# Making the head projections' weight sums on GpSimd from loaded blocks, and starting the MLP's sums and the second block's token loads later

## The chip, the cores and the metric

The kernel runs on one core of one Trainium2 chip. The metric is device time in microseconds of one execution; the median of three executions is 2469.45 us.

## The reference

One decoder layer on x of 2048 tokens by 1024 features in float32, then a final RMSNorm:

```python
h = rmsnorm(x, mix_norm_g[l])
proj = h @ w_in[l]
q, k, v, g, u = jnp.split(proj, [R, 2 * R, 3 * R, 4 * R], axis=-1)
y_ret = jax.nn.silu(g) * head_rmsnorm(retention(q, k, v, positions), ret_gn_g[l])
y_pool = pool_mixer(u, pool_w[l], pool_scale[l])
x = x + jnp.concatenate([y_ret, y_pool], axis=-1) @ w_out[l]
x = x + cross_attn(rmsnorm(x, xa_norm_g[l]), mem_n, xa_wq[l], xa_wkv[l], xa_wo[l])
x = x + conv_glu_ffn(rmsnorm(x, ffn_norm_g[l]), ffn_w_up[l], ffn_conv_w[l],
                     ffn_conv_b[l], ffn_w_down[l])
```

Retention has 4 heads of 128 (rotary q and k, decay, chunks of 128 tokens, a norm by head, a SiLU gate). The pooling mixer takes trailing means over 2, 4, 8 and 16 tokens in 4 groups. The cross-attention reads 256 memory tokens; the MLP has 2 x 2816 columns and a causal convolution of width 3 ahead of the gate.

## The kernel before

The sequence is worked through in two blocks of 1024 tokens (b = 0 and 1), features on the 128 partitions. A float32 matmul is made as three passes (`passes`, lines 271 to 273): each operand is split into a high part, which ScalarE writes (`act.activation` to the type fp32r), and a low part, which VectorE writes (the difference), and the passes are high by high, high by low and low by high. So every weight tile that TensorE reads is first loaded, then split by ScalarE and VectorE.

Projections with square blocks of weights use a scheme of seven products in place of eight. Three of the seven left operands are blocks of the weights, the other four are sums of blocks. For the head projections these are the arrays `Ad` (one entry for each of the 8 pairs of column groups in `PAIRS`), for the MLP `Ud` and `Dd`. `weight_sums` makes all of them in device memory, without any engine's arithmetic: GpSimd issues for each job four DMAs that copy and four that add while they write (lines 925 and 922). It is a generator; its jobs are advanced by turns, each with a small ScalarE copy (line 940) and a GpSimd copy (line 941) that tie the turn to a place in the order. `spacing` says how many calls make one turn. Turns are taken in the last steps of the prologue, between the value projections of block 0, in the head projections and in the later stages.

Block 0 then goes as follows. `folded_weights` (a generator, `todo` in the outer function, advanced by `folded(n)`) multiplies the attention's weights into the memory: first wkv and wqT (stores of `Md`, line 501), later pool weights and wo (stores of `WPd`, line 571, and `VWd`, line 591). `values` projects v. Beside it `rope_steps` makes the rotary tables on VectorE and ScalarE, and SP stores them (`rope0`, line 1903), and `quarter_sums` makes the sums of x for the seven products. `head_projections` makes q, k, the gates and the pool inputs: a `Heads` member for each pair fetches seven tiles of 128x512 (line 1020), into places of `raws` (seven places of 512 columns in R and S3), splits each (line 1636) into a place of `prs` (Q and S45) and multiplies it with a sum of x. It runs `retention` for the head before in between (`behind`), and `pool_steps` (`todo` inside it) for the pooled groups. What is left of both is done behind the last product (`finish()` and a loop), after which the outer function runs the rest of `folded`, four times with two `token_squares` of block 1 between (the second copy of x, `xR`, tokens on partitions; loaded by `load_tokens` at line 626, squared by ScalarE with a row sum at line 622). The output projection (`unit`, weights from `wout_r` and `WPd`) and the cross-attention follow.

Each engine runs its instructions in order. The written order is not that order: a scheduler with a model of time places each instruction on its engine, so that a change in one place can move rows elsewhere. SP issues most loads, in order, and a load waits in SP's queue until its place is free.

The head projections' fetch, and the rest behind block 0's heads:

```python
own = [sums[i][:, : halves * P] for i in range(4)]
self.loads = [part(0, 0), own[2], own[1], part(0, 1), own[0], own[3], part(1, 1)]
...
load_tokens(1, k, room)
folded(1)
for h in range(HEADS):
    for k in (2 * h, 2 * h + 1):
        token_squares(1, k, room, token_sums[:, KT:])
    folded(1)
```

Of the kernel before, what the change touches and what calls it, by code (L numbers as in the profile page):

```python
# [8 lines left out]
F32 = mybir.dt.float32  # L9
# [3 lines left out]
ALU = mybir.AluOpType  # L13
# [123 lines left out]
def trunk(ctx, tc, xT, xR, memT, pos, w_qkgu, w_v, wkv, wqT, wo, wout_r, wout_p, poolT, w_up, w_dn, vecs, consts, outT):  # L137
# [576 lines left out]
    def retention(b, h, qkg, v):  # L714
# [89 lines left out]
        yield  # L804
        a.mixed()
# [731 lines left out]
    def head_projections(b, v, rb, t1, t2, z, got):  # L1537
# [76 lines left out]
        class Heads(Member):  # L1614

            def __init__(self, p):
                super().__init__([w_qkgu[n] for n in PAIRS[p]], Ad[p], 0, 4)
                self.groups, self.how, self.seen, self.acc = PAIRS[p], [""] * 7, set(), None
                self.ended = []
# [68 lines left out]
        class Late:  # L1688
# [6 lines left out]

            def fetch(self, i):
# [49 lines left out]
        fetches, made, highs = list(items), [], []  # L1746
# [5 lines left out]
        def fill():  # L1752
# [3 lines left out]
            if len(made) < len(items) and prs.room():  # L1756
                m, i = items[len(made)]
                while i not in m.raw:
                    fetch()
# [5 lines left out]
        def step():  # L1765
            if todo and next(todo[0], True) is not None:
                todo.pop(0)

# [8 lines left out]
        for at, (m, i) in enumerate(items[:own]):  # L1777
# [18 lines left out]
            next(under[0], None)  # L1796
# [24 lines left out]
        S[0] = new_s(F32, 0)  # L1821
        raws = Places([(R, j * T) for j in range(3)] + [(r, 0) for r in S], T)
        prs = Places([(Q, j * T) for j in range(3)], T)
# [95 lines left out]
    for n in range(1, 2 * KT + HEADS):  # L1919
# [17 lines left out]
        if n > 2 * KT:  # L1937
            next(under[0])
        folded(1)
    reclaim(spare)  # L1940
    for b in range(NB):
# [9 lines left out]
        def between():  # L1951
            next(behind[0], None)
            place[0] += 1
            if b == 0 and place[0] % 2:
                next(under[0])
# [20 lines left out]
        else:  # L1976
# [28 lines left out]
        first = 0  # L2005
# [9 lines left out]
        for n in range(first, KT):  # L2015
# [4 lines left out]
            unit(raw, mixed, add_residual(b, n, xs, got=got), (0, 2, 3, 1, 4, 6, 7, 5) if b == 0 else range(KT))  # L2020
# [201 lines left out]
```

## Time and profile before

| what | us |
|---|---|
| median of three executions | 2469.45 (2468.44 to 2470.31) |
| the profiled execution's own time | 2470.04 |
| its span, first to last instruction | 2468.2 |
| TensorE busy in the span | 2403.8 (97%) |
| VectorE busy | 1717.3 (70%) |
| ScalarE busy | 1355.2 (55%) |
| GpSimd busy | 308.2 (12%) |
| bytes moved by DMA | 526.23 MB |

The span is what the trace holds; the execution's own time has 1.8 us more around it. PE is TensorE's matmuls, PEld its weight loads, DVE VectorE, ACT ScalarE, POOL GpSimd, SP the engine that issues most DMAs. A name with a q behind it is the engine's queue, which issues and waits. In a row of instructions, out<-in are tiles by name, and the bracket at the end holds the engine's idle time before it and what ended that.

### The profile page before, as it was taken

To read this page: it belongs to the slowest core of one execution; us is meant where nothing else is said; L and a number is where in the kernel's file an instruction comes from. 1 tells how busy PE (TensorE), PEld (TensorE's weight loads), DVE (VectorE), ACT (ScalarE), POOL (GpSimd) and SP (SyncE) were. 2 spreads that over 40 slices of the span, in tenths; PEclk is the share of its full clock that TensorE was granted. 3 is DMA by queue.
4 is the path that set the end of the run, shared out by engine and by line. 5 is a ranking of instruction groups with operands and counts; after the bars stand their busy time and mean duration, and the time that the engine had idled before them with its cause. 6 is when DMAs were issued, how large, how long until landed. Compare 5 with 4: busy or idle time off the path is not lost.

```text
span 2468.2 us, 33388 instructions
## 1 busy us (share of the span) xinstructions
PE 2403.8 (97%) x11186; PEld 2002.1 (81%) x11186; DVE 1717.3 (70%) x2872; ACT 1355.2 (55%) x2498; POOL 308.2 (12%) x477
## 2 busy tenths in 40 slices
PE   9779999999999999999999999999999999999998
PEld 8658877888888888888888888888888888888887
DVE  7366874564566775574678776897667688867876
ACT  7434565443345553434655555675555577666664
POOL 0245120315113300000000010020000000000000
PEclk9889998999999999999999999999999999999999
DMA  9999589949868744356568655665446468757952
GB/s 355 300 256 283 144 230 308 286 121 291 252 190 220 182 110 154 111 203 209 177 198 283 205 187 164 213 222 171 162 158 214 136 224 294 258 181 261 356 187 73
DMA packets 275581, 526.23 MB, mean 213 GB/s; under 512 B 30144, under 2 KB 59344, under 8 KB 275408
## 3 DMA queue, kind: packets, MB, share of 16 engines
q1 hardware_dynamic: 212768, 408.59, 49.7%
q0 software_dynamic: 37376, 86.00, 14.9%
q10 hardware_dynamic: 25264, 29.49, 3.4%
q8 instruction: 88, 1.44, 0.2%
q14 instruction: 85, 0.70, 0.1%
HBM read 420.68 MB, written 189.28 MB: 247 GB/s over the span
## 4 chain that ended last, share of the span: by engine, by line
PE 83%; DVE 1%; ACT 0%; issue 0%; DVEq 0%; ACTq 0%
PE mm L271 26%; PE mm L272 26%; PE mm L273 26%; PE aux L271 1%; PE aux L273 1%; PE aux L272 1%; PE aux L855 1%; DVE Z L243 0%; PE aux L363 0%; PE aux L765 0%; PE aux L763 0%; PE aux L735 0%; PE aux L747 0%; PE aux L778 0%; PE aux L737 0%; DVE T L243 0%
## 5 line engine op out<-in xcount | busy, mean ns | idle before, releaser
L271 PE MATMUL mm<-G,Q 128*128 128x512 f32 (+1 forms) x1665 | 642.1, 386 | 19.1 <-ACT Q L1636 10.4
L273 PE MATMUL mm<-G,Q 128*128 128x512 f32 (+1 forms) x1665 | 637.7, 385 | 2.3 <-DVE Q L243 2.3
L272 PE MATMUL mm<-G,Q 128*128 128x512 f32 (+1 forms) x1537 | 590.4, 384 | 0.4 <-DVE G L251 0.2
L272 PE MATMUL mm<-G,E 128*128 128x512 f32 (+1 forms) x1092 | 420.4, 385 | 0.0
L271 PE MATMUL mm<-G,E 128*128 128x512 f32 (+1 forms) x1092 | 418.8, 385 | 0.7 <-ACT E L259 0.7
L273 PE MATMUL mm<-G,E 128*128 128x512 f32 (+1 forms) x1092 | 418.3, 385 | 0.2 <-DVE E L243 0.2
L271 PEld LDWEIGHTS mm<-G,Q 128*128 128x128 f32 x1665 | 315.2, 189 | 84.0 <-ACT Q L1636 11.6
L273 PEld LDWEIGHTS mm<-G,Q 128*128 128x128 f32 x1665 | 314.8, 189 | 64.5 <-DVE Q L243 3.8
L272 PEld LDWEIGHTS mm<-G,Q 128*128 128x128 f32 x1537 | 291.1, 189 | 56.3 <-DVE G L243 1.2
L243 DVE TENSOR_TENSOR Z<-Z,mm 128x512 f32<-128x512 f32 (+1 forms) x322 | 215.0, 671 | 124.2 <-PE mm L273 122.7
L251 DVE SCALAR_TENSOR_TENSOR Z<-Z,vecs 128x1024 f32<-128x1024 f32 x176 | 224.4, 1279 | 50.2 <-ACT Z L1089 46.8
L271 PEld LDWEIGHTS mm<-G,E 128*128 128x128 f32 x1092 | 205.1, 188 | 41.9 <-ACT E L259 0.9
L273 PEld LDWEIGHTS mm<-G,E 128*128 128x128 f32 x1092 | 205.1, 188 | 41.5 <-DVE E L243 0.4
L272 PEld LDWEIGHTS mm<-G,E 128*128 128x128 f32 x1092 | 205.1, 188 | 41.1
L243 DVE TENSOR_TENSOR Q<-R,Q 128x512 fp32r<-128x512 f32 x180 | 122.5, 686 | 83.3 <-ACT Q L259 53.7
L1026 ACT ACTIVATE E<-R 128x512 fp32r<-128x512 f32 (+1 forms) x165 | 101.4, 615 | 141.1 <-PE mm L272 135.2
L243 DVE TENSOR_TENSOR T<-T 128x512 f32<-128x512 f32 (+4 forms) x196 | 134.1, 688 | 24.8 <-ACT T L432 12.4
L243 DVE TENSOR_TENSOR G<-T,G 128x512 fp32r<-128x512 f32 (+1 forms) x169 | 110.3, 672 | 38.4 <-ACT G L259 18.7
L973 ACT ACTIVATE G<-T 128x512 fp32r<-128x512 f32 x180 | 108.6, 623 | 40.5 <-DMA T<-Gd 30.4
L243 DVE TENSOR_TENSOR E<-R,E 128x512 fp32r<-128x512 f32 (+1 forms) x137 | 91.3, 671 | 54.9 <-ACT E L1026 39.3
L1089 ACT ACTIVATE Z<-Z,vecs 128x1024 f32<-128x1024 f32 x88 | 109.1, 1241 | 31.8 <-DVE Z L243 30.9
L1026 ACT ACTIVATE E<-S 128x512 fp32r<-128x512 f32 (+1 forms) x107 | 65.9, 616 | 106.7 <-PE mm L272 104.1
(348 smaller groups left out, 3917.8 us busy)
## 6 DMA issues: line engine op xcount, KB each, us to landing
T<-Gd SPq DMA_DIRECT2D x168, 256.0 KB, 4.7
Ud<-w_up POOLq DMA_DIRECT2D x132, 256.0 KB, 9.5
Gd<-Z SPq DMA_DIRECT2D x110, 256.0 KB, 2.8
R<-Ud SPq DMA_DIRECT2D x106, 256.0 KB, 2.7
R<-w_up SPq DMA_DIRECT2D x80, 256.0 KB, 3.1
S<-Ud SPq DMA_DIRECT2D x70, 256.0 KB, 2.9
Gd<-T SPq DMA_DIRECT2D x56, 256.0 KB, 3.3
T<-Xd SPq DMA_DIRECT2D x53, 256.0 KB, 4.1
```

Of the source, the lines that this page charges most:

```text
L243: return eng.tensor_tensor(out=out, in0=a, in1=b, op=op)
L251: return dve.scalar_tensor_tensor(out=out, in0=a, scalar=s, in1=b, op0=op0, op1=op1)
L271: pe.matmul(ps, lh, rh, start=start, stop=False, skip_group_check=more)
L272: pe.matmul(ps, lh, rl, start=False, stop=False, skip_group_check=more)
L273: latest[0] = pe.matmul(ps, ll, rh, start=False, stop=stop, skip_group_check=more)
L855: pe.transpose(tp[:, j * P : (j + 1) * P], e.f[:, j * P : (j + 1) * P], ident)
L973: one = act.activation(hi, x, AF.Copy, scale=-1.0 if i == 2 else 1.0)
L1026: act.activation(p2[:, 0, :w], self.raw[i].f[:, :w], AF.Copy)
L1089: act.activation(self.c[g].f, a[:, 2:], AF.Identity, bias=cb[:, f : f + 1], scale=cw[2][:, f : f + 1])
```

## The change

In block 0 the sums for the head projections are no longer taken from `Ad`. `Heads` loads the four raw blocks of a pair, and `summed` lets GpSimd add two places of `raws` into a third (for one sum in place), and store the sum to `Ad`, from where block 1 reads it as it did. `weight_sums` loses the eight jobs of `Ad`; the MLP's jobs, which stay, are not advanced in the prologue, in block 0's values or in its head projections any more. What is left of retention and of the pooled groups behind block 0's last product is interleaved with steps of `folded`; the places are set back to whole tiles ahead of that (`back`). The loads and squares of `xR` go into the loop of block 0's output projection, one for each unit. `retention` has one more `yield` ahead of the scores of heads 0 to 2, and one ahead of the last head's `mixed`. Block 0's output units take k = 3 last.

```diff
@@ retention
         both_ss, rr = small(8), small(8)
+        if h < HEADS - 1:
+            yield
...
         c.scaled(rr)
         yield
+        if h == HEADS - 1:
+            yield
         a.mixed()
@@ weight_sums
-        jobs = [((w_qkgu[a], w_qkgu[c]), 0, 4, Ad[p]) for p, (a, c) in enumerate(PAIRS)]
-        jobs += [((w_up[f], w_up[f + NF]), 0, 4, Ud[f]) for f in range(NF)]
+        jobs = [((w_up[f], w_up[f + NF]), 0, 4, Ud[f]) for f in range(NF)]
@@ head_projections, class Heads
+                if not b:
+                    a, c = (w_qkgu[n] for n in PAIRS[p])
+                    self.loads = {0: block((a, c), 0, 0, 0, 4), 4: block((a, c), 1, 0, 0, 4), 6: block((a, c), 1, 1, 0, 4), 3: block((a, c), 0, 1, 0, 4)}
+
+            def summed(self, i, x, y, at=None):
+                r = at or raws.take()
+                tt(pool, r.f, self.raw[x].f, self.raw[y].f, ALU.add)
+                pool.dma_start(self.to[(4, 2, 1, 5).index(i)], r.f)
+                self.raw[i] = r
+
+            def fetch(self, i):
+                if b:
+                    return super().fetch(i)
+                self.steps += 1
+                if i in (0, 1, 2, 5):
+                    super().fetch({0: 0, 1: 4, 2: 6, 5: 3}[i])
+                elif i == 3:
+                    self.summed(1, 4, 6)
+                    self.summed(4, 0, 4, self.raw[4])
+                elif i == 4:
+                    self.summed(2, 0, 1)
+                else:
+                    self.summed(5, 3, 2)
+
+            def ready(self, i):
+                return i in self.raw and (b or self.steps >= (5, 5, 7, 7, 4, 7, 4)[i])
...
-            next(under[0], None)
+            if b:
+                next(under[0], None)
...
-        finish()
+        if not b:
+            back()
+        while next(behind[0], True) is None:
+            if not b:
+                folded(1)
         while todo:
             step()
+            if not b:
+                folded(1)
@@ the outer function
-        if n > 2 * KT:
-            next(under[0])
...
-            if b == 0 and place[0] % 2:
-                next(under[0])
...
-            room = [Z.take() for _ in range(KT)]
-            for k in range(KT):
-                load_tokens(1, k, room)
-            folded(1)
-            for h in range(HEADS):
-                for k in (2 * h, 2 * h + 1):
-                    token_squares(1, k, room, token_sums[:, KT:])
-                folded(1)
-            for r in room:
-                r.free()
+            folded(100)
...
-            unit(raw, mixed, add_residual(b, n, xs, got=got), (0, 2, 3, 1, 4, 6, 7, 5) if b == 0 else range(KT))
+            if not b:
+                load_tokens(1, n, room)
+            unit(raw, mixed, add_residual(b, n, xs, got=got), (0, 1, 2, 4, 6, 7, 5, 3) if b == 0 else range(KT))
+            if not b:
+                token_squares(1, n, room, token_sums[:, KT:])
+                room[n].free()
```

How the built order moves, at three places. First the start of block 0's head projections. SP's queue there, before (xT is the load of `quarter_sums`, L1903 and L1565 store and load the rope tables, L1020 is the fetch of head weights):

```order
L1508 DMA S3_79<-xT 128x1024
L1508 DMA S2_78<-xT 128x1024
L1020 DMA R_76<-Ad_91 128x512
L1020 DMA R_76<-w_qkgu 128x512
L1508 DMA R_76<-xT 128x1024
L1903 DMA rope0_102<-T_75 128x512 x3
L1020 DMA R_76<-Ad_91 128x512
L1565 DMA Z1_74<-rope0_102 64x2x512 x2
L1020 DMA R_76<-w_qkgu 128x512
L1020 DMA S3_79<-Ad_91 128x512
L1565 DMA Z1_74<-rope0_102 64x2x512 x2
L1020 DMA R_76<-Ad_91 128x512 x2
```

SP's queue at the same place now (line 1511 is the load of xT, 1948 and 1568 the rope tables, 1023 the fetch):

```order
L1511 DMA S3_79<-xT 128x1024
L1511 DMA S2_78<-xT 128x1024
L1023 DMA R_76<-w_qkgu 128x512 x2
L1511 DMA R_76<-xT 128x1024
L1948 DMA rope0_102<-T_75 128x512 x2
L1023 DMA R_76<-w_qkgu 128x512
L1948 DMA rope0_102<-T_75 128x512
L1568 DMA Z1_74<-rope0_102 64x2x512 x2
L1023 DMA R_76<-w_qkgu 128x512
L1568 DMA Z1_74<-rope0_102 64x2x512 x2
L1023 DMA R_76<-w_qkgu 128x512
L1023 DMA S3_79<-w_qkgu 128x512 x2
```

Two raw blocks now stand ahead of the last xT and the rope stores, the third stands between the rope stores, and no load of Ad is left. ScalarE there, before (L709 evicts values, L681 and L683 are the sine and cosine, L1519 and L1534 belong to `quarter_sums`):

```order
L709 ACTIVATE Z1_74<-mm48_1394,rn17_518 128x4x128
L709 ACTIVATE Z1_74<-mm49_1395,rn17_518 128x4x128
L262 ACTIVATE G_72<-R_76,vecs_80 128x512
L681 ACT_TABLE_LOAD
L681 ACTIVATE T_75<-T_75 128x512
L1534 ACTIVATE G_72<-R_76 128x512
L683 ACTIVATE T_75<-T_75,consts_81 128x512
L1901 ACTIVATE T_75<-T_75 128x512
L1519 ACTIVATE T_75<-S3_79,vecs_80 128x512
L1534 ACTIVATE G_72<-Z1_74 128x512
L262 ACTIVATE G_72<-S3_79,vecs_80 128x512
L940 ACTIVATE halo_94<-consts_81 128x2
```

ScalarE now, around the sine (L1522, L1537 and L1946 are the lines that were 1519, 1534 and 1901):

```order
L709 ACTIVATE Z1_74<-mm46_1256,rn17_518 128x4x128
L709 ACTIVATE Z1_74<-mm47_1257,rn17_518 128x4x128
L262 ACTIVATE G_72<-R_76,vecs_80 128x512
L681 ACT_TABLE_LOAD
L681 ACTIVATE T_75<-T_75 128x512
L1537 ACTIVATE G_72<-R_76 128x512
```

and a few rows later, around the last two evictions of values (L1665 is the split of a head weight):

```order
L1537 ACTIVATE G_72<-S3_79 128x512
L1665 ACTIVATE Q_77<-R_76 128x512
L709 ACTIVATE Z1_74<-mm48_1319,rn17_518 128x4x128
L1537 ACTIVATE G_72<-Z1_74 128x512
L709 ACTIVATE Z1_74<-mm49_1320,rn17_518 128x4x128
L1665 ACTIVATE Q_77<-S3_79 128x512
```

The sine stood behind the last two evictions of values (mm48 and mm49) and now stands ahead of them, and the first split of a head weight stands ahead of both too.

Second, GpSimd's first instructions of the program's body, before:

```order
L941 COPY halo_94<-halo_94 128x2
L925 DMA Ad_91<-w_qkgu 128x512 x4
L941 COPY halo_94<-halo_94 128x2
L925 DMA Ad_91<-w_qkgu 128x512 x4
L922 DMA Ad_91<-w_qkgu 128x512 x2
L941 COPY halo_94<-halo_94 128x2
L922 DMA Ad_91<-w_qkgu 128x512
L925 DMA Ad_91<-w_qkgu 128x512 x4
L922 DMA Ad_91<-w_qkgu 128x512
L922 DMA Ad_91<-Ad_91 128x512
```

GpSimd now, from its first add on (L1630 stores a sum):

```order
L243 TENSOR_TENSOR S3_79<-R_76 128x512
L1630 DMA Ad_91<-S3_79 128x512
L243 TENSOR_TENSOR R_76<-R_76 128x512
L243 TENSOR_TENSOR S3_79<-R_76,S3_79 128x512
L1630 DMA Ad_91<-R_76 128x512
L1630 DMA Ad_91<-S3_79 128x512
L243 TENSOR_TENSOR R_76<-R_76,S3_79 128x512
L1630 DMA Ad_91<-R_76 128x512
L243 TENSOR_TENSOR R_76<-S3_79 128x512
L1630 DMA Ad_91<-R_76 128x512
```

The DMAs of the weight sums for the heads are gone from the prologue, and adds with a store each stand in the head projections; the first DMA of the MLP's sums comes behind all 32 of them.

Third, SP's queue in the tail of block 0's heads, before (L497 loads wout_p and wo, L626 loads xR):

```order
L497 DMA R_76<-wout_p 128x1024
L497 DMA S3_79<-wout_p 128x1024
L626 DMA Z1_74<-xR 128x1024
L497 DMA R_76<-wout_p 128x1024
L560 DMA R_76<-poolT 128x4x128
L577 DMA R_76<-Vd_104 128x2x512
L497 DMA R_76<-wo 128x1024
L497 DMA S3_79<-wo 128x1024
L577 DMA R_76<-Vd_104 128x2x512
L497 DMA S128_3062<-wout_p 128x1024
L497 DMA R_76<-wo 128x1024
L626 DMA Z1_74<-xR 128x1024 x2
```

SP's queue in the tail now:

```order
L497 DMA R_76<-wout_p 128x1024 x2
L560 DMA R_76<-poolT 128x4x128
L497 DMA S3_79<-wout_p 128x1024
L577 DMA R_76<-Vd_104 128x2x512
L497 DMA R_76<-wo 128x1024
L497 DMA S3_79<-wo 128x1024
L577 DMA R_76<-Vd_104 128x2x512
L497 DMA S126_2904<-wout_p 128x1024
L497 DMA R_76<-wo 128x1024 x3
L497 DMA S126_2904<-wo 128x1024
L497 DMA S3_79<-wo 128x1024
L2049 DMA R_76<-wout_r 128x512
```

The loads of xR are gone from between those of wo; they now stand among the x loads of the output projection.

More of the change, by code (lines that the diff above doesn't have):

```diff
@@ L1757, in fill @@
                 m, i = items[len(made)]
-                while i not in m.raw:
+                while not m.ready(i):
                     fetch()
@@ L1767, in step, with back @@
                 todo.pop(0)
+        def back():
+            nonlocal raws, prs
+            S[0] = new_s(F32, 0)
+            raws = Places([(R, j * T) for j in range(3)] + [(r, 0) for r in S], T)
+            prs = Places([(Q, j * T) for j in range(3)], T)
         while True:
@@ L1820, in head_projections @@
             fill()
[L1821 to L1823 removed]
+        if b:
+            back()
     def rows_norm(s_acc):
@@ L2003, in mixed @@
             return [r[:, s * SUB : (s + 1) * SUB] for r in mix[k][1]]
-        first = 0
+        first, room = 0, [] if b else [Z.take() for _ in range(KT)]
         if b:
```

7 lines of the change are left out of this document (5 added, 2 removed).

## Prediction

> **What bounds the kernel now.** I read the page's first two parts, then a table of busy time by stage, then TensorE's idle times one by one, and only then the other engines at those places.
>
> ```profile
> span 2468.2 us, 33388 instructions
> PE 2403.8 (97%) x11186; PEld 2002.1 (81%) x11186; DVE 1717.3 (70%) x2872; ACT 1355.2 (55%) x2498; POOL 308.2 (12%) x477
> PEclk9889998999999999999999999999999999999999
> ```
>
> TensorE is busy 97% of the span, so 64.4 us of idle time and the slices below 9 in the granted clock are all that a change of order can win. The stage table (columns: busy us of each engine, granted clock, DMA share, GB/s) says where they lie.
>
> ```profile
> core 0: us, PE busy (x) PEld busy (x) DVE busy (x) ACT busy (x) POOL busy (x), PEclk, DMA share, GB/s
> 60.00:97.00 37.00, 20.35 (x147) 18.99 (x146) 15.28 (x23) 21.68 (x49) 12.48 (x20) 0.86 0.94 314
> 97.00:147.00 50.00, 49.89 (x231) 41.53 (x230) 26.35 (x45) 16.17 (x35) 17.80 (x27) 0.96 0.97 251
> 147.00:180.00 33.00, 15.61 (x40) 11.55 (x41) 15.15 (x25) 12.88 (x24) 16.16 (x26) 0.69 0.93 260
> 180.00:335.00 155.00, 155.00 (x798) 131.78 (x797) 113.04 (x235) 79.17 (x184) 53.81 (x82) 1.00 0.82 217
> 335.00:402.00 67.00, 55.42 (x247) 42.32 (x246) 48.94 (x96) 50.96 (x112) 6.07 (x9) 0.87 0.88 282
> 402.00:500.00 98.00, 98.00 (x436) 81.15 (x434) 44.70 (x69) 40.20 (x74) 29.90 (x45) 1.00 1.00 292
> 500.00:900.00 400.00, 399.44 (x1931) 334.14 (x1931) 256.01 (x526) 188.91 (x413) 111.35 (x172) 1.00 0.73 199
> 900.00:1000.00 100.00, 96.69 (x451) 80.48 (x450) 56.76 (x104) 35.92 (x79) 0.00 (x0) 0.98 0.40 128
> ```
>
> Three stretches hold 45.6 us of idle TensorE: 60 to 97 (16.65, end of the folding before values), 147 to 180 (17.39, start of block 0's head projections) and 335 to 402 (11.58, their tail and the rest of the folding). The other 18.8 us lie outside, 3.31 of them in the last row. The DMA engines are nearly full, 0.88 to 0.97, in exactly these. The idle times one by one (start, duration, what ran, in brackets the idle time before it and what ended it):
>
> ```profile
> 94.48 0.58 PE L271 MATMUL mm<-G 128*128 128x256 f32 x1 [11.84 <-ACT G L259]
> 156.82 0.80 PE L271 MATMUL mm<-G,Q 128*128 128x512 f32 x1 [9.93 <-ACT Q L1636]
> 160.07 0.79 PE L273 MATMUL mm<-G,Q 128*128 128x512 f32 x1 [1.17 <-DVE Q L243]
> 173.84 0.79 PE L271 MATMUL mm<-G,S 128*128 128x512 f32 x1 [6.40 <-ACT S L1636]
> 367.95 1.32 PE L271 MATMUL mm<-G,Q 128*128 128x512 f32 x2 [3.72 <-ACT G L259]
> ```
>
> All wait for the first split of an operand or an eviction. A second cost follows: after such a gap the clock is granted at half.
>
> ```profile
> 94.40:100.70 6.30, 6.22 (x19) 5.25 (x20) 1.52 (x3) 0.55 (x2) 2.37 (x4) 0.50 0.99 299
> 156.80:165.60 8.80, 7.61 (x17) 5.54 (x18) 4.42 (x8) 1.01 (x2) 5.52 (x9) 0.51 0.96 223
> 173.80:179.20 5.40, 5.36 (x13) 4.20 (x14) 2.08 (x3) 2.09 (x5) 4.95 (x9) 0.50 1.10 254
> 367.90:380.70 12.80, 9.06 (x18) 5.42 (x19) 10.16 (x27) 9.38 (x20) 0.00 (x0) 0.51 0.85 281
> 397.30:401.10 3.80, 3.74 (x9) 2.97 (x10) 1.40 (x3) 3.54 (x8) 0.00 (x0) 0.55 1.10 377
> ```
>
> Busy time at half clock counts half: 6.22, 7.61, 5.36, 9.06 and 3.74 us lose some 3.1, 3.8, 2.7, 4.5 and 1.7, together 15.8. With the idle time, 61.4 us is the most that the three stretches can give.
>
> **Term 1, 60 to 97.** The old weight sums put 17 of GpSimd's DMAs here; the new ones put none.
>
> ```profile
> 87.68 0.93 ACTq L501 DMA_DIRECT2D Md<-T  x2
> 88.72 1.21 ACT L548 ACTIVATE T<-mm,vecs 128x256 f32<-128x256 f32 x3 [8.96 <-issue]
> q0 software_dynamic: 955, 2.68, 21.2%
> Ad<-w_qkgu POOLq DMA_DIRECT2D x16, 256.0 KB, 9.5
> Md<-T ACTq DMA_DIRECT2D x12, 256.0 KB, 10.8
> Xd<-T ACTq DMA_DIRECT2D x14, 256.0 KB, 2.2
> ```
>
> The first two rows show ScalarE held for 8.96 us in front of a store of Md that it could not issue. The next three are DMA rows of 55 to 97 us: the software queue (GpSimd's) takes 21.2% of the engines there, 8.9 us of 42, and a store of Md takes 10.8 us to land. The last is a store of the same size between 900 and 1000 us, without GpSimd's DMAs: 2.2 us. I take the hold as gone: 9 of the 11.84 us. The remaining 4.8 us of small gaps and some 3 us of the large one belong to ScalarE's splits and stay. A 3 us gap should leave the clock alone for the most part: 2.5 of 3.1. Term 1 is 11.5 (bounds: 3 if the loads of wqT and w_v come as late as now, 19.8 for everything).
>
> **Term 2, 147 to 180.** Two gaps with two causes.
>
> ```profile
> 110.69 0.49 DVE L247 TENSOR_SCALAR T<-T,consts 128x512 f32<-128x512 int32 x1 [14.77 <-DMA Md<-T]
> 131.62 0.34 SPq L1508 DMA_DIRECT2D R<-xT  x1
> 150.19 1.97 SPq L1903 DMA_DIRECT2D rope<-T  x3
> 155.09 0.63 ACT L1636 ACTIVATE Q<-R 128x512 fp32r<-128x512 f32 x1 [0.57 <-DMA R<-Ad]
> 173.16 0.63 ACT L1636 ACTIVATE S<-S 128x512 fp32r<-128x512 f32 x1 [15.35 <-DMA S<-w_qkgu]
> q0 software_dynamic: 5074, 12.11, 62.0%
> ```
>
> VectorE starts the rope tables at 110.69 after 14.77 us without work, waiting for loads. Its chain to the sine takes until SP can store the result at 150.19. SP's queue stands from 131.96 to 150.19 behind the store of that sine, and the head weights, an Ad among them, stand behind it; so the first product begins 9.93 us late. In the new order the first product needs a raw w_qkgu block that is loaded ahead of the rope stores, its split stands ahead of the last two evictions of values, and no Ad is loaded. VectorE's chain still has to be through, and I let 3 us stand: 8 of 9.93 + 1.17. The second gap is a 256 KB load that ScalarE awaits for 15.35 us while the software queue holds 62.0% of the DMA engines (the q0 row is of 97 to 180 us): all 6.4 go. Of the clock's 6.5 I take 5. Term 2 is 19 (bounds: 6, if the rope chain starts as late as now and only the second gap goes; 23.9).
>
> GpSimd now makes the operand of the second product: raw 6 comes behind two rope stores, then one add. The second product comes 2.7 us of matmuls after the first (12 of 112 in 25 us), and its load needs some 3; I count 0, since the first product waits for VectorE at the same time.
>
> **Term 3, 335 to 402.**
>
> ```profile
> 374.62 0.63 ACT L259 ACTIVATE G<-R 128x512 fp32r<-128x512 f32 x1 [2.42 <-DMA R<-wo]
> Z<-xR SPq DMA_DIRECT2D x8, 512.0 KB, 5.5
> R<-wo SPq DMA_DIRECT2D x4, 512.0 KB, 6.0
> ```
>
> TensorE's order here is the old one almost row for row; what changes is who else is on the queues. Eight loads of xR (4 MB), their squares on ScalarE and a turn of the weight sums leave this stretch. The loads of wo should come in some 3 us rather than 6.0. VectorE is 73% busy and stays so. I take half of 11.58 + 6.2: 9 (bounds 3 and 17.8).
>
> **What it costs.** GpSimd makes 32 sums of 128x512. No row shows an add on GpSimd; the nearest are these.
>
> ```profile
> L243 DVE TENSOR_TENSOR Q<-R,Q 128x512 fp32r<-128x512 f32 x180 | 122.5, 686 | 83.3 <-ACT Q L259 53.7
> L941 POOL COPY halo<-halo 128x2 f32<-128x2 f32 x45 | 31.1, 692 | 503.4 <-ACT halo L940 503.4
> L925 POOL DMA_DIRECT2D Ud<-w_up x88 | 59.6, 1066 | 18.8 <-DMA Ud<-w_up 11.1 <-DMA Ud<-Ud 3.8 <-DMA Ad<-w_qkgu 2.0
> ```
>
> At least 0.69 us as on VectorE; GpSimd's copy of two columns takes as long, so a fixed cost plus a pass gives 1.4, and I bound it at 2.8, twice that. Four adds and four issues of 1.07 make 10 us a pair (15.5 at the bound), and a pair has 7 x 12 matmuls, 18.75 us: GpSimd keeps up. The Trainium skill, "GPSIMD Engine Reference", section 3.1, gives 4497 ns for an add of 2048 columns, 1.96 times VectorE; by that an add here is an estimated 1.34 us and the sum is the same.
>
> Each sum sits in its place until its store has landed, and SP's next raw load waits for that place with all of SP's queue behind it. A split runs four products (10.7 us) ahead, stores take 2 to 9 us: cost 0, up to 5 if stores land late. VectorE is busy 113.04 of 155 us in 180 to 335, so 42 us of cover; I count 2 for collisions with the adds (0 to 10).
>
> The MLP sums that block 0's projections carry today run later, at the same pace; GpSimd is idle from 900 on, where the DMA share is 0.40, and takes them there: 0. The xR loads fall into 402 to 500 us, where the DMA share is 1.00 and TensorE has no gap: 4 MB more on 292 GB/s over 98 us is 14%. Weights are fetched units ahead, x one unit (10.7 us): I count 2 (0 to 12). Their squares, eight of about a microsecond, lie on a ScalarE busy 40 of 98. The extra yields around the last head move few rows; block 1's gap of 3.3 us in 900 to 1000 I leave: 0 (from -3 to +3). The unit order that puts k = 3 last costs 0 (-1 to +1), the same matmuls.
>
> **Sum.** 11.5 + 19 + 9 - 2 - 2 = 35.5 us. The profiled execution took 2470.04 us (span 2468.2 and 1.8 around it), 0.6 above the median of 2469.45; 2470.04 - 35.5 is 2434.5.
>
> **Rivals.**
> Everything in the three stretches goes: 61.4 less 2, 2411. For it: DMA waits stand behind each large gap. Against it: ScalarE is busy 59% and 76% of the first and third, and some gaps wait for its own work.
> The head start stays bound by VectorE: term 2 is 6, 2447.5. For it: VectorE is 15.15 of 33 us busy in that stretch, and its chain from 110.69 to 150 is long. Against it: the 14.77 us of idle time ahead of it.
> The traffic that is moved comes back as gaps in 402 to 500 and later: 15 us instead of 2, 2447.5. For it: the share of 1.00. Against it: no gap there now.
> Slower: GpSimd's adds and VectorE shut each other out in block 0's head projections. If each of the 32 adds holds VectorE for its whole time, 1.4 us gives 45 us against 42 of cover, about even; from 2.5 us an add (80 us, 38 over the cover) the whole gain is lost, and at 2.8 it is 2434.5 + 48 = 2482. Against it: only part of VectorE's work reads two SBUF tiles, and TensorE does not follow it at once. The Trainium skill, "SBUF — State Buffer", section "Who interferes with whom", speaks for this rival: a VectorE instruction with two SBUF inputs and a GpSimd instruction that reads SBUF exclude each other for the whole instruction. No run here shows it yet.
> The change does not do what it says, because the waits only take other names: 2468.
>
> **How the numbers follow.** My forecast 56% (2434.5, own range 2422 to 2446), everything goes 11%, VectorE's bound 14%, the moved traffic 11%, slower 4%, nothing 4%. 0.2%, 5 us, is about what a measurement here can tell from no change. So faster 0.92, same 0.04, slower 0.04. The range that leaves out less than 2 in 10 reaches over the middle cases and most of the first: 2414 to 2456.
>
> **What would show it.** Term 1: no gap over 4 us ahead of the first values, and Md landing in under 5 us. Term 2: no stretch at half clock between values and the second pair; rows of adds on GpSimd near 1.4 us. Term 3: no gap of 3 us before the first output unit. Costs: VectorE's mean for Q<-R,Q in the head projections (686 ns now) tells the collisions, gaps in the output projection the traffic. I am wrong if the adds take 2.5 us or more, or if the first head product still waits some 10 us for VectorE.

## The result and the profile after

The changed kernel takes 2445.35 us (median of four executions, 2443.56 to 2446.90), the kernel before 2469.57 beside it: 24.2 us less, a ratio of 0.9902 with a 95% interval from 0.9885 to 0.9919. The forecast was 35.5 us less. The profiled execution took 2443.56 us; its page begins so (span, busy time of the engines, granted clock in 40 slices):

```profile
span 2441.8 us, 33334 instructions
PE 2396.9 (98%) x11186; PEld 1997.9 (82%) x11186; DVE 1745.8 (71%) x2872; ACT 1351.5 (55%) x2488; POOL 323.2 (13%) x469
PEclk9999989999999999999999999999999999999999
```

The span is 26.4 us shorter. TensorE's idle time in it went from 64.4 to 44.9 us, which is 19.5; its busy time fell by 6.9 with the same 11186 matmuls, and the size of that fits the stretches at half clock, which cost 15.8 us before by the prediction's table and 6.8 now (half of 4.16 and of 9.52 in the rows below). The table by stage, at the same places of the program as the table of before:

```profile
core 0: us, PE busy (x) PEld busy (x) DVE busy (x) ACT busy (x) POOL busy (x), PEclk, DMA share, GB/s
55.00:93.00 38.00, 35.36 (x254) 33.46 (x253) 19.30 (x28) 27.91 (x60) 0.00 (x0) 0.96 0.93 332
130.00:156.00 26.00, 18.66 (x71) 14.12 (x70) 21.71 (x22) 8.56 (x15) 15.66 (x16) 0.87 0.55 167
156.00:305.00 149.00, 143.84 (x735) 121.52 (x734) 123.02 (x213) 70.58 (x163) 47.05 (x48) 0.99 0.26 86
305.00:370.00 65.00, 54.23 (x256) 43.57 (x255) 55.44 (x113) 50.12 (x109) 0.00 (x0) 0.89 0.59 181
370.00:468.00 98.00, 98.00 (x430) 80.02 (x429) 40.27 (x63) 43.10 (x79) 22.60 (x38) 1.00 0.94 293
```

Idle TensorE, before and after, by stretch: end of the folding before values 16.65 and 2.64 us; start of the head projections 17.39 and 7.34; the rest of them 0 and 5.16; tail 11.58 and 10.77; output projection 0 and 0. So the first stretch gave 14, the second 10, the tail under one, and a place that had no gap now has 5 us of them. The gaps one by one:

```profile
133.40 0.50 PE L273 MATMUL mm<-G,Q 128*128 128x512 f32 x1 [2.22 <-DVE Q L243]
141.64 0.80 PE L273 MATMUL mm<-G,Q 128*128 128x512 f32 x1 [5.09 <-DVE Q L243]
194.35 1.16 PE L735 MATMUL aux<-Z 128*128 128x128 f32 x8 [1.05 <-DVE Z L243]
261.35 0.49 PE L765 MATMUL aux<-T,Z 128*128 128x128 f32 x2 [3.13 <-DVE T L752]
349.40 0.79 PE L271 MATMUL mm<-G,Q 128*128 128x512 f32 x1 [4.43 <-ACT T L571]
```

The first four wait for VectorE, and none did so for more than 1.2 us before. The last is in the tail. Half the clock goes with the two larger ones, as it did before:

```profile
139.00:145.80 6.80, 4.16 (x10) 3.30 (x11) 5.59 (x7) 0.88 (x2) 2.56 (x4) 0.50 0.68 213
347.20:360.90 13.70, 9.52 (x25) 6.83 (x26) 13.07 (x32) 10.59 (x24) 0.00 (x0) 0.50 0.70 197
```

Why VectorE is late stands in its own rows beside GpSimd's. First VectorE from 134 to 143 us, and at 257:

```profile
134.00 5.26 DVE L243 TENSOR_TENSOR Z<-Z,T 128x512 f32<-128x512 f32 x2
139.19 2.40 DVE L243 TENSOR_TENSOR Q<-S,Q 128x512 fp32r<-128x512 f32 x1
142.71 0.68 DVE L243 TENSOR_TENSOR Q<-R,Q 128x512 fp32r<-128x512 f32 x1
256.92 3.45 DVE L243 TENSOR_TENSOR E<-E,Z 128x512 f32<-128x512 f32 x1
```

GpSimd's adds at the same times:

```profile
136.19 1.30 POOL L243 TENSOR_TENSOR R<-R 128x512 f32<-128x512 f32 x1
137.41 1.29 POOL L243 TENSOR_TENSOR S<-R,S 128x512 f32<-128x512 f32 x1
139.75 1.27 POOL L243 TENSOR_TENSOR R<-R,S 128x512 f32<-128x512 f32 x1
257.32 2.49 POOL L243 TENSOR_TENSOR R<-R 128x512 f32<-128x512 f32 x2
```

A sum of two tiles takes VectorE 0.68 us when GpSimd is quiet. Beside an add it takes 2.40, and the one at 256.92 takes 3.45: it lasts until both of GpSimd's adds behind one another are over. The surplus (1.72 and 2.77 us) is a little more than the adds themselves take (1.27 and 2.49). In the head projections 22 VectorE instructions exceed the median of their kind by more than 0.3 us, by 28.9 us together (added up from the trace over 130 to 305 us; a kind is one line and one pair of tiles). The four gaps above lie behind such rows.

A second thing shows at the start of the head projections. The rope tables' first instruction on VectorE now comes 18 us sooner than at 110.69. What it waits for is seen in the loads of positions that it reads; the second of them, with its us to landing, in the kernel before (issued at 97.77):

```profile
T<-pos SPq DMA_DIRECT2D x1, 128.0 KB, 12.7
```

In the changed kernel (issued at 88.62):

```profile
T<-pos SPq DMA_DIRECT2D x1, 128.0 KB, 3.9
```

And VectorE's row in the changed kernel:

```profile
92.63 0.49 DVE L247 TENSOR_SCALAR T<-T,consts 128x512 f32<-128x512 int32 x1 [10.54 <-issue]
```

Before, the load lands at 110.50 and VectorE starts 0.19 us later; now it lands at 92.55 and VectorE starts 0.08 later. In both kernels SP issues that load just when a store of Md has landed (97.75 and 88.61), since the load needs that store's place in T.

### The profile page after: what moved, and what is told of

It is laid out like the page before. It is cut to its first block, busy times and chain, and to the rows that moved or that the text cites. A ratio compares the mean times of both kernels' runs of the same rounds, so it can differ in the third digit from the quotient of the medians.

```text
span 2441.8 us, 33334 instructions
## 1 busy us (share of the span) xinstructions
PE 2396.9 (98%) x11186; PEld 1997.9 (82%) x11186; DVE 1745.8 (71%) x2872; ACT 1351.5 (55%) x2488; POOL 323.2 (13%) x469
## 4 chain that ended last, share of the span: by engine, by line
PE 92%; DVE 4%; ACT 2%; issue 1%; DMA 1%; SPq 0%; ACTq 0%; DVEq 0%
PE mm L271 29%; PE mm L272 29%; PE mm L273 29%; DVE Z L243 1%; DVE T L243 1%; PE aux L271 1%; PE aux L273 1%; PE aux L272 1%; PE aux L859 1%; DVE Q L243 1%; PE aux L765 1%; PE aux L763 1%; ACT R L1696 0%; PE aux L735 0%; PE aux L747 0%
## 5 line engine op out<-in xcount | busy, mean ns | idle before, releaser
L243 DVE TENSOR_TENSOR Q<-R,Q 128x512 fp32r<-128x512 f32 x180 | 128.2, 717 | 64.4 <-ACT Q L259 34.0
L243 DVE TENSOR_TENSOR T<-T 128x512 f32<-128x512 f32 (+4 forms) x196 | 135.6, 696 | 25.1 <-ACT T L432 12.4
```

The lines of the kernel that those rows point to most:

```text
L243: return eng.tensor_tensor(out=out, in0=a, in1=b, op=op)
```

## Experiments

All times are medians beside runs of the kernel before on the same chip (2467.7 to 2469.6 in every comparison); the ratios to it are what is compared. A difference in us between two experiments is given by their medians; by the ratios it comes out up to 1.6 us otherwise.

**The sums on VectorE.**

```diff
-                tt(pool, r.f, self.raw[x].f, self.raw[y].f, ALU.add)
+                tt(dve, r.f, self.raw[x].f, self.raw[y].f, ALU.add)
```

> The changed kernel with the 32 sums made by VectorE instead of GpSimd (the stores stay on GpSimd's queue). Theory A: in the changed kernel an add on GpSimd shuts VectorE out; VectorE's instructions beside the adds take 28.9 us longer than their medians, and TensorE's new gaps of 5.1 us (at 136), 3.1 us (258), 1.1 and 0.6 us (193, 171) with the half clock behind the first two are its price. Adds on VectorE cost 32 x 0.69 = 22 us there, spread one by one; the four gaps shrink to under 2 us in sum, no VectorE instruction of that stretch takes over 1.5 times its median, and the time is 2445 - 6 to 12 = 2433 to 2439. Theory B: VectorE is simply full at these places (123 of 149 us busy), whoever adds; then 22 us more of adds leave the gaps as they are or longer: 2445 to 2452.

2438.16 us, ratio 0.9879 (0.9865 to 0.9892): 7.2 us under the changed kernel by the medians and 5.7 by the ratios, though the two intervals just overlap. In place of the row at 141.64 above stands the first of these, in place of the one at 261.35 the third:

```profile
139.87 0.50 PE L273 MATMUL mm<-G,Q 128*128 128x512 f32 x1 [2.28 <-DVE Q L243]
161.15 0.79 PE L271 MATMUL mm<-G,Q 128*128 128x512 f32 x1 [2.12 <-DVE T L243]
257.42 1.16 PE L747 MATMUL aux<-Z,T 128*128 128x128 f32 x8 [0.78 <-ACT T L741]
```

The two stretches of the heads in rows of the stage table:

```profile
130.00:156.00 26.00, 20.86 (x75) 15.96 (x74) 15.96 (x27) 8.69 (x15) 4.53 (x8) 0.87 0.53 162
156.00:305.00 149.00, 146.09 (x747) 123.75 (x748) 120.98 (x248) 73.26 (x167) 13.24 (x24) 0.99 0.27 87
```

VectorE now makes 32 adds more and is still sooner through: where 28.9 us of excess stood, no instruction exceeds its median by more than 0.3 us. Theory A holds in its sign and, at the low end, in its size, but not that the gaps shrink to under 2 us in sum: 7.3 us of them stay between 130 and 165, all on VectorE, and the changed kernel has 7.3 us there too. So at the start of the heads the idle time does not depend on who adds: VectorE, busy 15.96 of the first 26 us, is late there and not full, which is against Theory B's reason. The gain lies behind 165 us, where TensorE's idle time falls from 5.2 to 0.8 us.

**Each add twice.** The other direction, as a price.

```diff
                 tt(pool, r.f, self.raw[x].f, self.raw[y].f, ALU.add)
+                if at is None:
+                    tt(pool, r.f, self.raw[x].f, self.raw[y].f, ALU.add)
```

> The changed kernel with each sum that is not made in place added twice on GpSimd (24 more adds of 1.3 us, same values). Theory A (the adds shut VectorE out): VectorE's excess over its medians in the head projections goes from 28.9 us to 45 to 60, the gaps of TensorE there grow by 6 to 15 us: 2451 to 2460. Theory B (VectorE is full, GpSimd's adds do not matter): GpSimd is busy 47 of 149 us there and has room; 2445 within 3.

2464.69 us, ratio 0.9984 (0.9975 to 0.9993): 24 more adds cost 19.3 us. VectorE's excess is 48.2 us. The gaps at 141.64 and 261.35 have grown:

```profile
146.40 0.80 PE L273 MATMUL mm<-G,Q 128*128 128x512 f32 x1 [6.22 <-DVE Q L243]
282.08 0.49 PE L765 MATMUL aux<-T,Z 128*128 128x128 f32 x2 [4.05 <-DVE T L752]
```

GpSimd was idle for most of the stretch and had room. Its sums do come later: ScalarE's longest wait for one grows from 3.07 to 4.76 us. But of TensorE's 24.9 us of gaps between 130 and 300 us only 3.0 wait for ScalarE, 1.75 of them for a split of a head weight, and the others wait for VectorE; so it is in the main the exclusion and not GpSimd's own pace. The cost is above the 6 to 15 us expected, since new gaps with half clock came too. The Trainium skill, "SBUF — State Buffer", section "Who interferes with whom", has the rule: a VectorE instruction with two SBUF inputs and a GpSimd instruction that reads SBUF exclude each other for the whole instruction. The rows agree, 0.68 against 2.40 and 3.45 us; here an add that is added costs 0.8 us of the kernel (19.3 us by 24).

**The MLP's turns back in the prologue and in the values.**

```diff
+        if n > 2 * KT:
+            next(under[0])
@@ between
+            if b == 0 and place[0] % 2:
+                next(under[0])
```

> The changed kernel with the turns of the MLP's weight sums put back into the last steps of the prologue and between the value projections (not into the head projections). Theory A (GpSimd's DMAs held the stores of Md and the loads behind them): the gap ahead of the first values comes back at 8 to 12 us with a stretch at half clock, a store of Md lands in 8 to 11 us again; the head start is later too: 2445 + 12 to 25 = 2457 to 2470. Theory B (the gap went because instructions were reordered, not because of the traffic): 2445 within 3.

2492.62 us, ratio 1.0098 (1.0085 to 1.0112): 47 us more than the changed kernel, about twice the most that was expected. The gap ahead of the values is back (10.39 us), and so is one of 9.43 us ahead of the first head product; the next experiment has both too, and costs 20 us. The other 27 us are in the head projections: GpSimd's queue is in order, and its first add now stands behind DMAs of the MLP's sums that wait for one another. The stretch in a row of the stage table:

```profile
130.00:215.00 85.00, 58.24 (x203) 44.12 (x202) 50.94 (x83) 27.52 (x48) 50.07 (x71) 0.80 1.00 253
```

GpSimd's first add in order of time, and what stands before it:

```profile
165.76 0.52 POOL L928 DMA_DIRECT2D Ud<-w_up  x1 [1.47 <-DMA Ud<-w_up]
166.38 1.28 POOL L243 TENSOR_TENSOR S<-R 128x512 f32<-128x512 f32 x1
```

The first add comes at 166.38 us, 11 us after the last raw block that it needs has landed (155.25); it comes at 132.83 in the changed kernel, and at 154.38 with the turns of the prologue alone, so 12 us of the delay belong to the turns between the values. TensorE idles 26.8 of 85 us. Once GpSimd makes sums that TensorE waits for, its DMA turns ahead of them have to go elsewhere: these two parts of the change belong together.

**The turns back in the prologue alone.** Three turns; the trace shows 17 DMAs of them (an expectation below says 24, which is too many).

```diff
+        if n > 2 * KT:
+            next(under[0])
```

> The changed kernel with turns of the MLP's sums put back into the last three steps of the prologue alone. Theory A (the traffic there is what held the stores of Md): a gap of 8 to 11 us ahead of the first values and a half clock behind it, 12 to 17 us, and nothing else beyond 3 us: 2457 to 2465; the run sums_early then lost the rest, some 30 us, because GpSimd's adds stood behind DMAs on its queue. Theory B (the gap needs the turns in the values too): 2445 within 4.

2465.38 us, ratio 0.9989 (0.9980 to 0.9998). 20 of the 24 us are gone, and not for the first gap alone. TensorE:

```profile
92.61 0.58 PE L271 MATMUL mm<-G 128*128 128x256 f32 x1 [10.02 <-ACT G L259]
153.00 0.80 PE L271 MATMUL mm<-G,Q 128*128 128x512 f32 x1 [9.43 <-ACT Q L1665]
```

The rope tables' first instruction on VectorE:

```profile
107.67 0.49 DVE L247 TENSOR_SCALAR T<-T,consts 128x512 f32<-128x512 int32 x1 [13.62 <-DMA Md<-T]
```

The second load of positions, and the stores of Md from 55 to 97 us:

```profile
T<-pos SPq DMA_DIRECT2D x1, 128.0 KB, 11.4
Md<-T ACTq DMA_DIRECT2D x12, 256.0 KB, 10.1
```

Both large gaps of the kernel before are back, with the raw blocks and the adds, and but for one place with the order of SP's loads as changed. The second opens 34 us after the last of those DMAs has landed (109.69). Expected was the first gap only.

**The kernel before without those three turns.** The mirror image, with no other part of the change.

```diff
-        if n > 2 * KT:
-            next(under[0])
```

> The kernel before, with one edit: the three turns of the weight sums in the last steps of the prologue are left out, so that the same jobs start with the first values. All sums, Ad too, are still made by GpSimd's DMAs. Theory A (these 24 DMAs hold the stores of Md; the stores hold places of T; the rope tables wait for the places, and so VectorE and the head start are late): the gap of 11.84 us ahead of the values goes, VectorE's first rope instruction comes at some 92 us instead of 110.7, and 10 to 20 us are gained without a single add on GpSimd: 2448 to 2459. What may be given back: Ad is made later, and the first head products may wait for it. Theory B (it takes the raw blocks and GpSimd's adds to start the heads early): the first gap goes, but Ad's later DMAs delay the heads by as much: 2463 to 2470.

2443.01 us, ratio 0.9899 (0.9882 to 0.9915): as much as the whole change, by leaving out two lines. More than Theory A's 10 to 20 us. VectorE's first rope instruction:

```profile
92.64 0.49 DVE L247 TENSOR_SCALAR T<-T,consts 128x512 f32<-128x512 int32 x1 [10.59 <-issue]
```

And the largest gap that stays at the start of the heads, on ScalarE and TensorE:

```profile
150.94 0.63 ACT L1636 ACTIVATE S<-S 128x512 fp32r<-128x512 f32 x1 [11.02 <-DMA S<-w_qkgu]
151.62 0.80 PE L271 MATMUL mm<-G,S 128*128 128x512 f32 x1 [7.84 <-ACT S L1636]
```

VectorE starts the rope tables at 92.64, as in the changed kernel (92.63), and the first head product comes at 131.30 (130.44 in the changed kernel, 156.82 before). What stays there is mainly a gap of 7.84 us, for a raw block that took 12.4 us to land beside the DMAs that make Ad. The expectation, which spoke of places of T, was half right: the last thing that VectorE waits for is the load of positions, here too (it lands at 92.56), and the place is what that load's issue waits for. The turns consist of DMAs and of small copies on ScalarE and GpSimd, and this run leaves out both; that it is the DMAs is read from the times to landing, 12.7 and 11.4 us for the load of positions with the turns and 3.9 and 4.0 without.

**The second copy of x back in the tail.**

```diff
+            room = [Z.take() for _ in range(KT)]
+            for k in range(KT):
+                load_tokens(1, k, room)
+            folded(1)
+            for h in range(HEADS):
+                for k in (2 * h, 2 * h + 1):
+                    token_squares(1, k, room, token_sums[:, KT:])
+                folded(1)
             folded(100)
+            for r in room:
+                r.free()
...
-            if not b:
-                load_tokens(1, n, room)
             unit(raw, mixed, add_residual(b, n, xs, got=got), (0, 1, 2, 4, 6, 7, 5, 3) if b == 0 else range(KT))
-            if not b:
-                token_squares(1, n, room, token_sums[:, KT:])
-                room[n].free()
```

> The changed kernel with the eight loads of the second copy of x and their squares put back behind block 0's heads, where the kernel before has them. Theory A (as predicted: this traffic delays the loads of wo): wo lands in 6.0 us instead of 4.6, and the tail takes 3 to 9 us more: 2448 to 2454. Theory B (the tail is held by VectorE, busy 55 of 65 us there, and by the few places for wo): 2445 within 2, and since nothing is moved into the output projection, perhaps 1 us less.

2451.00 us, ratio 0.9930 (0.9918 to 0.9943): 5.7 us. That is Theory A's size, though the loads of wo are not what it goes through: they land in 4.5 and 5.0 us (medians of the tiles S and R; 4.6 in the changed kernel). What comes back is a gap at the end, behind an eviction of VWd, where nothing stood:

```profile
387.37 0.79 PE L271 MATMUL mm<-Q,G 128*128 128x512 f32 x1 [3.28 <-ACT T L591]
```

**The tail not interleaved; the yields and the unit order undone.** Two kernels.

```diff
-        while next(behind[0], True) is None:
-            if not b:
-                folded(1)
+        finish()
         while todo:
             step()
-            if not b:
-                folded(1)
```

> The changed kernel with the rest of retention and of the pooled groups first and the rest of the folding behind it, not interleaved step by step; the second copy of x stays in the output projection. Theory A (as predicted, TensorE's order in the tail is the old one almost row for row, the interleaving itself is worth nothing): 2445 within 3. Theory B (the interleaving gives TensorE and the loads of wo work beside each other's waits): the tail takes 3 to 10 us more, 2448 to 2455.

2446.15 us, ratio 0.9914 (0.9900 to 0.9928).

```diff
-        if h < HEADS - 1:
-            yield
...
-        if h == HEADS - 1:
-            yield
         a.mixed()
...
-            unit(raw, mixed, add_residual(b, n, xs, got=got), (0, 1, 2, 4, 6, 7, 5, 3) if b == 0 else range(KT))
+            unit(raw, mixed, add_residual(b, n, xs, got=got), (0, 2, 3, 1, 4, 6, 7, 5) if b == 0 else range(KT))
```

> The changed kernel without the two extra yields in retention and with the old order of block 0's output units. Theory A (as predicted, both are worth nothing): 2445 within 3. Theory B (the yields keep retention's VectorE work away from the first splits of a pair, and the unit order lets the first units start while k = 3 is still being made): 2449 to 2455.

2444.73 us, ratio 0.9904 (0.9891 to 0.9918). Neither is to be told from the changed kernel: these parts are worth nothing that a run shows.

**The tail's evictions on VectorE.** On top of adds_vector.

```diff
-                act.activation(t.f[:, :SUB], ps, AF.Copy)
+                dve.tensor_copy(t.f[:, :SUB], ps)
```

> The sums on VectorE, and the eight evictions of WPd (line 571) made by VectorE instead of ScalarE. Theory A (the tail's largest gap, 4.0 us in adds_vector, and the half clock behind it come because these evictions stand on ScalarE behind a split that waits for a load of wo): the gaps on line 571 go from 6.1 us to under 2, the half clock stretch of 13.7 us shrinks: 2438 - 5 to 10 = 2428 to 2433. Theory B (the load itself is the limit, TensorE waits for the next weights right behind): the gap takes another name, 2438 within 3. Theory C (VectorE, busy 55 of 65 us there, is the limit): 2438 + 0 to 4.

2442.52 us, ratio 0.9895 (0.9880 to 0.9910), by the medians 4 us more than adds_vector. The gaps keep their line and change the engine:

```profile
344.31 0.77 PE L271 MATMUL mm<-G,Q 128*128 128x512 f32 x1 [4.06 <-DVE T L571]
```

The tail in a row of the stage table:

```profile
299.00:361.00 62.00, 50.17 (x236) 39.07 (x235) 56.40 (x116) 42.96 (x95) 0.00 (x0) 0.89 0.55 166
```

VectorE is busy 56.40 of 62 us there, ScalarE 42.96. Theory A is wrong: the gap did not come from ScalarE's queue alone. Theory C, VectorE as the limit, fits best, but the intervals of the two runs overlap, and Theory B, in which the gap only takes another name, is not excluded.

**The rope tables earlier.** On top of adds_vector, from four steps before the end of the prologue, and from one.

```diff
+    early = rope_steps(0)
     for n in range(1, 2 * KT + HEADS):
...
         if n >= 2 * KT:
             wv.append(value_weights(n - 2 * KT, B.arenas[(n - 2 * KT) // 2]))
+            next(early)
...
-        tables = iter(()) if b else rope_steps(0)
+        tables = iter(()) if b else early
```

> The sums on VectorE, as in the run adds_vector, and the rope tables of block 0 begun in the last four steps of the prologue instead of between the value projections. Theory A (what is left of the head start's loss, gaps of 2.2, 2.3, 0.6 and 2.1 us with 10 us at half clock, is VectorE's queue, which is full from 92 to 133 us because it sat idle for 10.6 us before its first rope instruction at 92.3): the first split of a head weight comes some 8 us sooner, the gaps of 130 to 160 go to under 2 us in sum: 2438 - 6 to 11 = 2427 to 2432. Theory B (the rope tables take places of T that the stores of Md need, and ScalarE's splits stand behind them): the gap ahead of the values comes back, 2438 + 0 to 8.

2439.97 us, ratio 0.9884 (0.9867 to 0.9902), nothing against adds_vector. Both theories were at work. Between 130 and 156 us TensorE is busy for all 26 us, and ahead of the values four gaps on the evictions of Md came instead:

```profile
130.00:156.00 26.00, 26.00 (x117) 21.52 (x116) 13.48 (x22) 11.17 (x20) 2.17 (x4) 1.00 0.46 142
```

The first and the last of the four gaps:

```profile
82.91 0.38 PE L271 MATMUL mm<-G,Q 128*128 128x256 f32 x1 [3.23 <-ACT T L548]
95.42 0.39 PE L271 MATMUL mm<-G 128*128 128x256 f32 x1 [1.52 <-ACT T L548]
```

So with `next(early)` only ahead of the last step (`if n == 2 * KT + HEADS - 1`):

> The sums on VectorE, and the rope tables begun ahead of the last step of the prologue alone (rope_early began them four steps ahead). Theory A (rope_early won the head start, 7 us of gaps and 10 us at half clock, and lost as much ahead of the values, because six places of T were missing for four steps of Md stores): with one step most of the head start's gain stays and the gaps ahead of the values are under 3 us: 2438 - 4 to 9 = 2429 to 2434. Theory B (the places are missed in the last step as much, or VectorE starts no sooner than at 92): 2438 within 3.

2425.74 us, ratio 0.9829 (0.9814 to 0.9843): 12.4 us under adds_vector (4 to 9 were expected) and 19.6 under the changed kernel, the fastest kernel here. VectorE starts 4 us sooner, at the landing of positions, and the start of the head projections (117 to 143 us here) has no gap:

```profile
88.58 0.49 DVE L247 TENSOR_SCALAR T<-T,consts 128x512 f32<-128x512 int32 x1 [6.27 <-DMA T<-pos]
```

That stretch in a row of the stage table:

```profile
117.00:143.00 26.00, 26.00 (x117) 21.52 (x116) 22.51 (x37) 15.37 (x27) 3.76 (x7) 1.00 0.47 150
```

**The same without sums on any engine.** The kernel before, without the prologue's turns, with the rope tables ahead of the last step, and with the second copy of x and the unit order as changed.

> The kernel before with three edits and no sum on any engine: the three turns of the weight sums in the prologue are left out (as in before_no_turns), the rope tables begin ahead of the last step of the prologue (as in rope_last), and the loads and squares of the second copy of x go into the output projection with the changed unit order. Ad is still made by GpSimd's DMAs. Theory A (taking Ad's DMAs off the queues still pays at the head start: in before_no_turns a raw block took 12.4 us to land beside them and TensorE stood 7.84 us at 143): that gap and its half clock stay, 2426 + 6 to 13 = 2432 to 2439. Theory B (with VectorE early, the heads' loads are early too, and DMAs instead of adds cost nothing): 2426 within 4.

2445.67 us, ratio 0.9904 (0.9887 to 0.9920): 20 us slower than rope_last, more than Theory A's 6 to 13. TensorE's gaps:

```profile
143.49 0.79 PE L271 MATMUL mm<-G,S 128*128 128x512 f32 x1 [6.17 <-ACT S L1636]
166.14 0.79 PE L271 MATMUL mm<-G,Q 128*128 128x512 f32 x1 [4.10 <-DVE T L243]
```

DMA rows of 130 to 160 us, with us to landing at the end:

```profile
R<-Ad SPq DMA_DIRECT2D x4, 256.0 KB, 11.9
Z<-rope SPq DMA_DIRECT2D x4, 256.0 KB, 14.0
```

With GpSimd's DMAs in the head start, the load of a rope table takes 14.0 us (3.9 in rope_last), and VectorE, early as it was, waits for it. Until 171.87 us GpSimd's DMAs make Ad alone, so both of these gaps lie beside Ad's DMAs and not beside the MLP's. The two kernels also differ in the tail's interleaving and the yields, which showed nothing above, and in the MLP's turns behind 171.87. So keeping the DMAs that make Ad out of the head start, with the sums on an engine instead, is worth up to 20 us once VectorE starts early and is not held by GpSimd's adds.

## Why the prediction was right, and where its steps failed

The sign was right, and 2445.35 us lies in the range that was given for the forecast itself (2422 to 2446), but at its very edge. The sum was 11 us too large, one cause was named wrongly, and errors of both signs cancelled in part: the measured terms below, 16.5 + 14.5 + 2.2 - 7.2, make 26.0 us, beside 26.5 between the two profiled executions.

- **Term 1 (11.5, bounds 3 to 19.8): too small.** 14.0 us of idle time went; with the clock, the first eviction of values comes 16.5 us sooner (111.57, now 95.09). I left 4.8 us of small gaps and 3 of the large one to ScalarE; only 2.6 stayed. That a store of Md would land in under 5 us was wrong: it takes 7.1 (10.8 before), and that is enough. Nor are full DMA engines the mark of the stretches with gaps, as the prediction read its table: 402 to 500 us had a share of 1.00 and no gap, and the first stretch keeps 0.93 (0.94 before) with 14 us less idle time. What changed is whose DMAs they are: none of GpSimd's is left there.
- **Term 2 (19, bounds 6 to 23.9): 14.5, and by another mechanism.** 10.05 us of idle time and 4.4 of clock (6.5 before, half of 4.16 now). The step that failed is "the first product needs a raw w_qkgu block that is loaded ahead of the rope stores, ... and no Ad is loaded" as the reason for the first gap. In before_no_turns Ad is loaded and the order is the old one, and this gap is gone; in sums_prologue there is no Ad and the gap is there. It is VectorE's chain, as the prediction's own row at 110.69 said, and that chain hangs on the same 17 DMAs as term 1, by the positions' load. The second gap was read rightly: GpSimd's DMAs, 7.84 us in before_no_turns.
- **Term 3 (9, bounds 3 to 17.8): too large.** By the stage tables 0.8 us of idle time and 1.4 of clock (6.2 before, half of 9.52 now), by the run that moves the loads back 5.7; why the two differ was not settled. Loads of wo took 4.6 us and not the 3 that I took. The tail's gaps wait for ScalarE and VectorE.
- **Collisions (2, bounds 0 to 10): mis-sized.** 7.2 us against adds_vector by the medians, 5.7 by the ratios. I had priced an add about rightly (1.4 us; 1.27 to 1.30 in the rows above) and set 42 us of VectorE's idle time against them. That cover is a sum over 155 us and did not lie where the adds fell: behind 165 us TensorE followed VectorE directly. The largest gap came where VectorE had been 85% busy for 37 us (31.55 us between 93 and 130), but there the idle time is the same with the sums on VectorE. VectorE's mean for Q<-R,Q rose, as the sign that I had named: from 686 to 717 ns over the whole execution, to 881 in the heads (130 to 305 us).
- **The traffic (2), the stores, the yields and the unit order (0 each):** the first is 0 too, with no gap in 370 to 468 us; the others are as forecast.

The rival by which the head start stays bound by VectorE (2447.5) came nearest to the time, by luck: it has a term 2 of 6 us with a rope chain as late as before, where 14.5 us were measured with the chain 18 us sooner. It is right in that the 7.3 us of gaps that stay there wait for VectorE. The moved traffic, with the same 2447.5, did not show. The rival of exclusion was the right mechanism; its 48 us are for adds of 2.8 us, and for adds of 1.4 it said about even, where some 6 to 7 us were measured.

The balance is odd: the changed kernel (0.9902) and before_no_turns (0.9899) are equal. So leaving the 17 DMAs out of the prologue was shown to be enough for the whole gain, and putting such DMAs back takes 20 of the 24 us; the rest of the change paid for itself and no more. TensorE's idle times show where. At the start of the heads before_no_turns has 10.9 us between 130 and 165, mostly the wait beside Ad's DMAs, and the changed kernel 7.3, all on VectorE; behind that 0 and 5.2, the collisions; in the tail 14.0 (310 to 385) and 10.8. So the wait for Ad was for the most part exchanged for one for VectorE.

## What to carry to other kernels

Follow a late engine back past the first waiter: two gaps 60 us apart had one cause, a burst of DMAs that delayed stores, whose places a small load needed, which a long VectorE chain needed. Before moving arithmetic to GpSimd, look for stretches in which TensorE follows VectorE directly, not at VectorE's mean; an add beside a VectorE sum of two tiles stops it for the whole burst. And try the smallest part of a large change by itself: two lines were worth as much as all of it.

## What was not expected of the hardware

- DMAs on GpSimd's queue stretched others far: behind 17 of 256 KB in the prologue, the last of which were still under way, a load of 128 KB took 12.7 us instead of 3.9; beside those that make Ad a raw block of 256 KB took 12.4 instead of 3.0 (median of eight in rope_last).
- Adds of GpSimd that follow one another hold VectorE through all of them, though VectorE's instruction is recorded as started first. VectorE in the changed kernel:

```profile
189.00 3.49 DVE L243 TENSOR_TENSOR R<-R,Z 128x512 f32<-128x512 f32 x1
```

GpSimd's pair:

```profile
189.40 2.53 POOL L243 TENSOR_TENSOR R<-R 128x512 f32<-128x512 f32 x2
```

The instruction that takes 0.68 us alone starts 0.40 us ahead of the pair and ends behind it, at 192.49; so it is at 257 us (256.92 and 257.32). Whether GpSimd's start is recorded late is open.
